# Differential attention in a hand-written matmul order, with the layer's last projections between its blocks

## The chip, the cores and the metric

The program runs on one core of a Trainium2 chip. The metric is the device time of one execution in microseconds (us). The engines are named as in the profile: PE (TensorE; PEld its weight loads), DVE (VectorE), ACT (ScalarE), POOL (GpSimd) and SP (SyncE, which issues the DMAs here).

## What is computed

A block of three branches (RWKV, convolution, memory attention) runs first; then two layers of this form, on a sequence of 1024 rows of width 1024. The change touches only these two layers.

```
for layer in range(2):
    h = rms_norm(x, norm_pre[layer])
    proj = h @ w_in[layer]                       # 4128 columns
    (gq, gk, gv, gg, gaf, gab, dq, dk, dv, dg, hq, hzf, hzb, hi, hg) = split(proj)
    y_a = gla_branch(...)                        # a scan forward and one backward, norm, * silu(gg)
    y_b = diff_branch(dq, dk, dv, dg, ...)
    y_c = hgrn_branch(...)                       # two scans, norm, * silu(hg)
    x = x + rms_norm(concat([y_a, y_b, y_c]) @ w_out[layer], norm_post[layer])

def diff_branch(q, k, v, g, ...):                # 4 heads, each with two pairs q, k of width 64
    q, k = rope(q) * 64**-0.5, rope(k)
    for each block of 128 queries:
        p = softmax(q @ k^T)                     # both pairs, over all 1024 keys
        w = p[0] - lam * p[1]
        o = w @ v                                # v is 128 wide
    o = rms_norm(o, norm_w) * (1 - lambda_init)
    return o * silu(g)
```

## The kernel before

Everything is float32. A projection is split in high and low parts, three matmuls for one (`mm3`): weights `whi` and `wlo` (made by ACT and by DVE or POOL from `wraw`), activations `hh` and `hl` in `hT`. One projection makes 128 columns for 1024 rows in two halves of 512; a half is 24 matmuls of 128x512 into one PSUM bank of the pool `fl`, and an evacuation follows: `p_func` copies it out by ACT, `p_rope` by ACT, then DVE and POOL, and `p_silu_le` reads the bank three times (ACT, DVE, DVE at its end). The result goes to DRAM.

A layer is `layer()`: six projections first, then `scans()`, `diff()` and the layer's output (`layer_out`, which reads all of `hT`). The other projections are a queue, `layer_stream`, from which `Stream.burst()` gives a part of one: `step` = 4 of the 8 row blocks, 12 matmuls, called a burst here. `scans()` has three scans (GLA, two pairs of HGRN heads); each has `scan_levels` (many small matmuls `aps`) and `scan_out` (state, outputs `ops`, norm sums `fst` in `finish_head`). Within these the PE order is pinned (`pinned`, `pin`: program order), and bursts stand between, all but each 14th call (`SKIP`). `reach(n)` runs the queue until n items are left. What remains at the end is fed at once by `stream.feed(1000)`, unpinned. Where nothing is pinned, a planner that runs when the program is built sets each engine's order. Scan outputs go to DRAM as float32 (`d_y`).

`diff()` then runs 32 blocks: four heads (`attend` twice per head) of eight blocks of 128 queries. A block is `weights` (eight score matmuls `sc` of 128x512 with the helper tiles `qz`, two maxima on DVE, two exps on ACT into `p`, a reciprocal and two combining steps on DVE), then eight transposes `wt` in two halves with two ACT copies into `wT`, then eight products `o_ps`. Four blocks make a half; it is normed (four squares on ACT, then Ln, Exp and a DVE product), transposed (`otp`), gated and put in `hT` as high and low parts. The next head's operands are loaded and split by `diff_qk` and `diff_v`, and between the halves `split_in` loads the scan outputs and splits them into `hT`. PSUM: two tiles for scores, three for `wt`, one for `o_ps`. Nothing of this is pinned.

## Time and profile before

| what | value |
|---|---|
| three runs | 3854.43, 3858.89 and 3860.61 us |
| median | 3858.89 us |
| profiled execution | 3856.55 us, span 3854.7 us |
| PE busy | 3531.4 us, 92% |
| layer 0: scans / rest to the layer's output | 348.21 / 232.13 us |
| layer 1: scans / rest to the layer's output | 350.14 / 239.70 us |

The median is 2.3 us longer than the profiled execution. A window is a stretch of the span in us, with each engine's busy time in it, the mean granted clock of PE (1.00 is 2.4 GHz), and the share and rate of DMA. A group puts instructions of one line and form together. A wait is idle time of an engine, with the instruction whose end released it.

### The profile page before, as it was taken

The numbers are of one execution on the slowest core, as the hardware profiler recorded it, in microseconds if no ns is written. First come the engines' busy times: TensorE is split into PE (matmuls) and PEld (weight loads), VectorE is DVE, ScalarE is ACT, GpSimd is POOL, SyncE is SP. The second block draws the span as 40 slices with busy tenths as digits, with TensorE's granted clock in tenths as the row PEclk, the third lists the DMA queues.
The fourth block names the chain that finished last, engine by engine and source line by source line (L and its number), as shares of the span: only waits on it lengthen the run. The fifth ranks groups of instructions, "written<-read, shape, count | busy, mean of one in ns | idle before, by whom it ended". The sixth has DMA issues, their size and how long they took to land. (4 is left out here: it accounts for less than half of the span.)

```text
span 3854.7 us, 69637 instructions
## 1 busy us (share of the span) xinstructions
PE 3531.4 (92%) x27522; PEld 2766.1 (72%) x27522; DVE 2330.0 (60%) x4505; ACT 1898.7 (49%) x3445; POOL 824.4 (21%) x710
## 2 busy tenths in 40 slices
PE   7999999999999999998999999899889999898887
PEld 5877766667666667766788767677777677677776
DVE  4346677777767767655454545465784544665863
ACT  4334544444444444445342445564674444655762
POOL 1002333333333333332122300012211300022111
PEclk9999999999999999999999999999999999999898
DMA  4421222222222222236554452323201442323113
GB/s 149 148 91 60 87 79 82 76 79 76 84 71 87 79 84 78 86 122 220 191 170 139 140 170 99 111 81 102 93 31 62 148 133 83 105 97 104 53 38 108
DMA packets 222584, 394.63 MB, mean 102 GB/s; under 512 B 24624, under 2 KB 44080, under 8 KB 222128
## 3 DMA queue, kind: packets, MB, share of 16 engines
q1 hardware_dynamic: 222256, 390.17, 30.4%
q8 instruction: 216, 3.54, 0.4%
q14 instruction: 112, 0.92, 0.1%
HBM read 268.44 MB, written 121.63 MB: 101 GB/s over the span
## 5 line engine op out<-in xcount | busy, mean ns | idle before, releaser
L250 PE MATMUL ps<-hh,whi 128*128 128x512 f32 (+2 forms) x3056 | 1280.5, 419 | 30.1 <-DVE st L202 11.8
L250 PE MATMUL ps<-hh,wlo 128*128 128x512 f32 (+2 forms) x3056 | 1200.4, 393 | 5.0 <-DVE wlo L202 4.9
L250 PE MATMUL ps<-hl,whi 128*128 128x512 f32 (+2 forms) x3056 | 1199.0, 392 | 4.2 <-DVE hl L202 4.2
L250 PEld LDWEIGHTS ps<-hh,whi 128*128 128x128 f32 (+1 forms) x3056 | 581.2, 190 | 198.7 <-issue 30.5
L250 PEld LDWEIGHTS ps<-hh,wlo 128*128 128x128 f32 (+1 forms) x3056 | 581.5, 190 | 137.8 <-DVE wlo L202 6.8
L250 PEld LDWEIGHTS ps<-hl,whi 128*128 128x128 f32 (+1 forms) x3056 | 583.1, 191 | 130.9 <-issue 19.7
L199 ACT ACTIVATE whi<-wraw 128x512 fp32r<-128x512 f32 x486 | 302.6, 625 | 556.9 <-PE ps L250 430.9
L202 DVE TENSOR_TENSOR wlo<-wraw,whi 128x512 fp32r<-128x512 f32 x398 | 296.5, 749 | 384.6 <-ACT whi L199 344.1
L202 POOL TENSOR_TENSOR uacg<-uacg,ut 128x512 f32<-128x512 f32 x240 | 339.0, 1413 | 781.5 <-ACT ut L569 646.2
L202 POOL TENSOR_TENSOR st<-st,rope 128x512 f32<-128x512 f32 x64 | 91.5, 1449 | 861.8 <-DVE st L415 855.0
L199 ACT ACTIVATE st<-ps 128x512 f32<-128x512 f32 (+2 forms) x260 | 149.3, 574 | 242.1 <-PE ps L250 213.4
L573 DVE SCALAR_TENSOR_TENSOR uacc<-uh,vecs,uacc 128x512 f32<-128x512 f32 x224 | 205.8, 919 | 8.1 <-ACT uacc L565 7.2
L202 POOL TENSOR_TENSOR acc<-acc,sq 128x512 f32<-128x512 f32 (+1 forms) x91 | 126.0, 1393 | 296.5 <-ACT sq L199 295.2
L202 POOL TENSOR_TENSOR wlo<-wraw,whi 128x512 fp32r<-128x512 f32 x88 | 121.0, 1375 | 287.1 <-ACT whi L199 260.3
L1387 DVE TENSOR_REDUCE D<-sc 128x1 f32<-128x1024 f32 x128 | 154.6, 1220 | 36.4 <-PE sc L250 36.1
L569 ACT ACTIVATE ut<-uh,vecs 128x512 f32<-128x512 f32 x240 | 166.0, 715 | 4.4 <-POOL uacg L202 3.7
L199 ACT ACTIVATE p<-sc,D 128x1024 f32<-128x1024 f32 x128 | 142.5, 1114 | 37.9 <-DVE D L1387 37.0
L250 PE MATMUL o_ps<-h,wT 128*128 128x128 f32 x1024 | 134.8, 280 | 12.9 <-ACT wT L199 12.9
L250 PEld LDWEIGHTS o_ps<-h,wT 128*128 128x128 f32 x1024 | 128.9, 195 | 22.6 <-ACT wT L199 17.5
L250 PE MATMUL sc<-h,h 128*128 128x512 f32 x256 | 96.3, 458 | 43.1 <-ACT p L199 43.1
L1380 POOL CAST qz<-h 64x128 fp32r<-64x128 f32 x128 | 53.8, 420 | 315.4 <-PE sc L250 309.0
L250 PE MATMUL ps<-oh,wlo 128*128 128x512 f32 x256 | 103.8, 406 | 4.6 <-DVE wlo L202 4.6
(331 smaller groups left out, 5885.4 us busy)
## 6 DMA issues: line engine op xcount, KB each, us to landing
wraw<-in_w_in_dram SPq DMA_DIRECT2D x326, 256.0 KB, 2.8
wraw<-in_w_out_dram SPq DMA_DIRECT2D x76, 256.0 KB, 2.7
g<-st SPq DMA_DIRECT2D x48, 256.0 KB, 2.2
y<-st SPq DMA_DIRECT2D x48, 256.0 KB, 2.0
gt<-y SPq DMA_DIRECT2D x48, 256.0 KB, 3.0
wraw<-in_w_mem_kv_dram SPq DMA_DIRECT2D x32, 256.0 KB, 2.9
yp<-gt SPq DMA_DIRECT2D x32, 256.0 KB, 3.3
yt<-yp SPq DMA_DIRECT2D x32, 256.0 KB, 3.1
```

What stands on the lines that cost most here:

```text
L199: self.nc.scalar.activation(out=out, in_=in_, func=func, **kw)
L202: (eng or self.nc.vector).tensor_tensor(out=out, in0=a, in1=b, op=op)
L250: self.pin(self.nc.tensor.matmul(out, lhsT=lhsT, rhs=rhs, start=start, stop=stop))
L569: keep(nc.scalar.activation(out=t, in_=u[:, j:j + 512], func=AF.Copy, scale=w(j)))
L573: keep(nc.vector.scalar_tensor_tensor(out=acc, in0=u[:, k:k + 512], scalar=w(k), in1=acc, op0=ALU.mult, op1=ALU.add))
L1380: nc.gpsimd.tensor_copy(out=Qz[slot][c][HEADS[c]], in_=Qs[c][HEADS[c], ts_])
L1387: nc.vector.reduce_max(out=D[:, c:c + 1], in_=sc, axis=AX.X, negate=True)
```

## The change

The queue of projections no longer ends ahead of the attention. `scans()` stops it at eight left (a `NEED` table says how many may be left at which place; `SKIP` is 4), and `diff(l, stream)` runs the rest in bursts of six matmuls (`step` = 2), pinned between its own. All matmuls of the attention are pinned too. Scores are written two blocks ahead (`LOOK`), so six `p` tiles are kept. PSUM in the attention: one bank for projections, two for `wt` instead of three. Two of the four gates of the attention (`g2`, `g3`) come later in the queue, and `g4` and `g5` last. `hT` is needed by projections to the end of the queue, so scan outputs and early heads are split at once and stored in DRAM as two tensors (`keep_out`), and `kept()` loads them into `hT` once the queue is empty. The rope tables are loaded again in the attention. The norm of a half is now one DVE product, one square, a DVE sum and a POOL product.

```diff
-FIRST, SKIP, PV = 6, 14, 5
+FIRST, SKIP, PV = 6, 4, 5
-NEED = 10
+NEED = dict(scan=18, qk=14, v=13, scans=8, heads=(5, 2), gates=(1, 0))
+LOOK = 2
...
-        for hd in range(4):
-            yield S(DG + hd, f"g{2 + hd}")
         for hd in range(4):
...
             yield P(DV + hd, f"d{hd}v")
+            for j in {1: (0, 1), 3: (2, 3)}.get(hd, ()):
+                yield S(DG + j, f"g{2 + j}")
...
+    def keep_out(self, p, o, j, sl):
+
+        hi, lo = p.tile([128, 512], F32, tag="fr", name="yhi", bufs=2).bitcast(R32), o.bitcast(R32)
+        self.act(hi, o)
+        self.lo(lo, o, hi)
+        for d, t in zip(self.d_y, (hi, lo)):
+            self.nc.sync.dma_start(out=d[j, :, sl], in_=t.bitcast(F32))
...
-            p1, p2, p3 = pool("d1", 1), pool("d2", 2), pool("d3", 5)
-            opp, wtp, scp = pool("dop", 1, space=PSUM), pool("dwt", 3, space=PSUM), pool("dsc", 2, space=PSUM)
+            p1, p2, p3 = pool("d1", 1), pool("d2", 2), pool("d3", 2 * LOOK + 2)
+            opp, wtp, scp = pool("dop", 1, space=PSUM), pool("dwt", 2, space=PSUM), pool("dsc", 2, space=PSUM)
+            self.fl = pool("dfl", 1, space=PSUM)
+            self.rot = self.rope(p1, ("rot0", "rot1"))
+            self.step, self.pinned = 2, True
...
-                for tt in range(4):
-                    self.act(o[:, tt], o_ps[:, tt], AF.Square, scale=D[:, tt, 4:5], accum_out=r[:, tt:tt + 1])
+                self.mul(o, o_ps, four(D[:, :, 4]))
+                self.act(q, o, AF.Square)
+                nc.vector.reduce_sum(out=r[:, 0:4], in_=q, axis=AX.X)
                 self.act(r[:, 4:8], r[:, 0:4], AF.Ln, scale=1.0 / 128, bias=self.eps(0))
                 self.act(r[:, 4:8], r[:, 4:8], AF.Exp, scale=-0.5)
-                self.mul(r[:, 4:8], r[:, 4:8], D[:, :, 4])
-                self.mul(o, o_ps, r[:, 4:8].rearrange("p (n o) -> p n o", o=1).to_broadcast([128, 4, 128]))
+                self.mul(o, o, four(r[:, 4:8]), eng=nc.gpsimd)
+                return o
...
                 self.stt(g, tp, nw, g, ALU.mult, ALU.mult)
-                self.put(self.hT[2 + hd], sl, g)
...
+                if stream.q or stream.g:
+                    self.keep_out(p1, g, 2 + hd, sl)
+                    waits.append((2 + hd, sl))
+                else:
+                    self.put(self.hT[2 + hd], sl, g)
+
+            def kept():
+                for j, sl in [(j, sl) for j in LAST[:4] for _, sl in self.halves()] + waits:
+                    for d, t in zip(self.d_y, self.hT[j]):
+                        nc.sync.dma_start(out=t[:, sl].bitcast(F32), in_=d[j, :, sl])
...
+            for b in range(LOOK):
+                ahead(b)
+                share(2 * b + 2)
+            pending = None
+            o_ps, held_back = None, True
+            for b in range(32):
+                hd, half, tt = b // 8, b // 4 % 2, b % 4
+                if b + LOOK < 32:
+                    ahead(b + LOOK)
+                goal = 4 + (b + 1) * 44 / 18 if b < 18 else 48 + 2 * (b - 17)
+                share((done + goal) / 2)
+                wT = turned(P.pop(b))
+                if pending and tt == 1:
+                    if pending[1] >= 2:
+                        reach(NEED["gates"][pending[1] - 2])
+                    out(*pending)
+                    pending = None
+                share(goal)
...
+                for kt in range(8):
+                    self.mm(o_ps[:, tt], wT[:, kt], vt[:, kt], kt == 0, kt == 7)
+                if tt == 3:
+                    pending = normed(o_ps, Ds[b // 4]), hd, slice(half * 512, half * 512 + 512)
...
+                if held_back and not (stream.q or stream.g):
+                    kept()
+                    held_back = False
+            out(*pending)
+            self.step, self.pinned = 4, False
...
                 if i == 0:
                     stream.reach(left)
+                elif i == 1:
+                    stream.reach(NEED["scan"])
...
-            self.pinned = False
-            self.head0 = qk, self.diff_v(0, l, self.qt, "t")
-            stream.feed(1000)
+            stream.reach(NEED["v"])
+            self.head0 = qk, self.diff_v(0, l, None, self.qt, "t")
+            stream.reach(NEED["scans"])
+            self.pinned = False
...
-                    nc.sync.dma_start(out=self.d_y[j, :, sl], in_=o)
+                    self.keep_out(p1, o, j, sl)
```

What this moves is seen on PE and DVE. First PE, some blocks into the first head of layer 0's attention, before; `sc` are scores, `wt` transposes, `o_ps` products:

```order
L250 MATMUL o_ps<-h_26249,wT 128x128 x8
L253 MATMUL wt<-const,p 128x128 x8
L250 MATMUL sc<-h_25769,h_25767 128x512 x2
L250 MATMUL sc<-h_25770,qz_26558 128x512 x2
L250 MATMUL sc<-h_25768,h_25766 128x512 x2
L250 MATMUL sc<-h_25770,qz_26559 128x512 x2
L250 MATMUL o_ps<-h_26249,wT 128x128 x8
```

In the changed kernel PE has this in the same head (`ps` are projections):

```order
L253 MATMUL ps<-hh_101,whi 128x512
L253 MATMUL ps<-hl_102,whi 128x512
L253 MATMUL ps<-hh_101,wlo 128x512
L256 MATMUL wt<-const,p 128x128 x8
L253 MATMUL ps<-hh_87,whi 128x512
L253 MATMUL ps<-hl_88,whi 128x512
L253 MATMUL ps<-hh_87,wlo 128x512
L253 MATMUL ps<-hh_89,whi 128x512
L253 MATMUL ps<-hl_90,whi 128x512
L253 MATMUL ps<-hh_89,wlo 128x512
L253 MATMUL o_ps<-h_25971,wT 128x128 x8
L253 MATMUL sc<-h_25523,h_25521 128x512 x2
```

Before, one block's transposes follow the last one's products at once, and the scores stand between them and their own products; now six projection matmuls stand ahead of the transposes and six more between them and the products, and the scores behind the products are those of two blocks later.

Then PE in the last quarter of layer 0's attention in the changed kernel, where the queue is empty:

```order
L253 MATMUL o_ps<-h_27578,wT 128x128 x8
L253 MATMUL sc<-h_27491,h_27489 128x512 x2
L253 MATMUL sc<-h_27493,qz_26033 128x512 x2
L253 MATMUL sc<-h_27492,h_27490 128x512 x2
L253 MATMUL sc<-h_27493,qz_26034 128x512 x2
L256 MATMUL wt<-const,p 128x128 x8
L256 MATMUL otp<-const,os 128x128 x4
L253 MATMUL o_ps<-h_27578,wT 128x128 x8
```

No projection stands between transposes and products there, and the output's transposes `otp` stand between them in one block of four.

Last DVE, at the gating of a half in layer 0's attention, before; `D<-sc` are maxima, `ld` is the gated half:

```order
L1387 TENSOR_REDUCE D<-sc 128x1
L202 TENSOR_TENSOR or<-or,D 128x4
L202 TENSOR_TENSOR os<-o_ps,or 128x512
L1387 TENSOR_REDUCE D<-sc 128x1
L1391 RECIPROCAL D<-D 128x2
L208 SCALAR_TENSOR_TENSOR ld<-otp,nw,ld 128x512
L208 SCALAR_TENSOR_TENSOR D<-D,lt 128x1
L208 SCALAR_TENSOR_TENSOR p<-p,D 128x1024
```

And in the changed kernel, where a silu's two DVE steps (`st`) now pass there:

```order
L211 SCALAR_TENSOR_TENSOR ld<-otp,nw,ld 128x512
L205 TENSOR_TENSOR ld<-ld,yhi 128x512
L211 SCALAR_TENSOR_TENSOR st<-ps,st 128x512
L1407 TENSOR_REDUCE D<-sc 128x1 x2
L205 TENSOR_TENSOR st<-st,ps 128x512
L1411 RECIPROCAL D<-D 128x2
L211 SCALAR_TENSOR_TENSOR D<-D,lt 128x1
L211 SCALAR_TENSOR_TENSOR p<-p,D 128x1024
```

Two maxima stand between the silu's first step and its product, which is the last read of the projection's bank; the split of the gated half (`ld` and `yhi`) stands ahead of both.

## Rows read from the trace of the kernel before

**Rows 1.** Page, part 1: busy time, share and instructions of each engine.

```profile
PE 3531.4 (92%) x27522; PEld 2766.1 (72%) x27522; DVE 2330.0 (60%) x4505; ACT 1898.7 (49%) x3445; POOL 824.4 (21%) x710
```

**Rows 2.** Windows by stage: from:to, length, busy time of each engine (instructions), clock, DMA.

```profile
2341.94:2690.15 348.21, 323.59 (x4138) 257.52 (x4138) 200.54 (x323) 195.52 (x307) 35.53 (x24) 0.98 0.28 94
2690.15:2922.28 232.13, 200.02 (x1235) 171.97 (x1234) 173.67 (x247) 165.49 (x350) 35.56 (x72) 0.96 0.18 59
3143.24:3493.38 350.14, 322.61 (x4137) 256.82 (x4137) 206.22 (x331) 195.07 (x307) 35.52 (x24) 0.98 0.28 93
3493.38:3733.08 239.70, 206.26 (x1235) 176.31 (x1234) 173.58 (x247) 165.53 (x350) 38.53 (x72) 0.93 0.17 58
```

**Rows 3.** Windows inside layer 0: first levels, first outputs, other scans, tail, start-up, blocks.

```profile
2341.94:2437.84 95.90, 92.28 (x1210) 73.53 (x1210) 46.23 (x75) 42.29 (x66) 0.00 (x0) 0.96 0.23 79
2437.84:2506.70 68.86, 55.46 (x794) 43.06 (x792) 36.09 (x53) 49.30 (x75) 0.00 (x0) 0.94 0.39 126
2506.70:2690.15 183.45, 175.85 (x2138) 140.94 (x2138) 118.22 (x195) 103.93 (x168) 35.53 (x24) 0.99 0.26 90
2690.15:2723.80 33.65, 33.65 (x153) 27.70 (x152) 11.36 (x22) 9.33 (x18) 11.65 (x12) 1.00 0.33 114
2723.80:2744.50 20.70, 13.61 (x56) 10.14 (x55) 18.71 (x27) 18.14 (x32) 2.64 (x7) 0.84 0.39 130
2744.50:2918.60 174.10, 152.26 (x1026) 133.62 (x1024) 142.74 (x197) 136.01 (x291) 21.26 (x53) 0.97 0.12 40
```

**Rows 4.** Windows inside layer 1: start-up of the attention, and its blocks.

```profile
3527.04:3548.40 21.36, 13.45 (x53) 10.07 (x51) 17.49 (x25) 16.89 (x30) 3.10 (x6) 0.72 0.37 127
3548.40:3729.50 181.10, 158.74 (x1030) 138.14 (x1028) 143.90 (x199) 137.31 (x293) 23.77 (x54) 0.94 0.12 40
```

**Rows 5.** Window in layer 0's tail, projection matmuls on PE alone.

```profile
2693.00:2720.00 27.00, 26.97 (x118) 1.00 0.29 96
```

**Rows 6.** Window of one block of attention without a gap on PE.

```profile
2749.88:2754.39 4.51, 4.51 (x35) 1.00 0.17 60
```

**Rows 7.** PE's waits, layer 0's scans, then attention: total, times, longest, us.

```profile
PE fst L250 <- ACT fr L199: 11.9, 2, 10.5
PE ps L250 <- DVE st L202: 5.2, 2, 3.6
...
PE sc L250 <- ACT p L199: 21.2, 14, 3.1
PE o_ps L250 <- ACT wT L199: 6.1, 7, 1.5
PE otp L253 <- DVE os L202: 3.3, 2, 3.2
```

**Rows 8.** Groups in layer 0's blocks: xcount | busy us, mean ns | idle.

```profile
L1387 DVE TENSOR_REDUCE D<-sc 128x1 f32<-128x1024 f32 x57 | 68.6, 1219 | 14.0 <-PE sc L250 13.9
L199 ACT ACTIVATE p<-sc,D 128x1024 f32<-128x1024 f32 x58 | 64.5, 1113 | 17.0 <-DVE D L1387 16.5
L208 DVE SCALAR_TENSOR_TENSOR p<-p,D 128x1024 f32<-128x1024 f32 x30 | 38.5, 1284 | 0.9
L199 ACT ACTIVATE wT<-wt 128x512 f32<-128x512 f32 x62 | 34.9, 597 | 13.5 <-PE wt L253 13.4
L202 DVE TENSOR_TENSOR h<-st,h 64x512 fp32r<-64x512 f32 x17 | 11.8, 693 | 2.9 <-ACT h L199 2.5
```

**Rows 9.** Timeline: start us, us, engine; first and last step of one silu.

```profile
2515.93 0.60 ACT L199 ACTIVATE st<-ps 128x512 f32<-128x512 f32 x1 [0.70 <-PE ps L250]
...
2519.72 0.68 DVE L202 TENSOR_TENSOR st<-st,ps 128x512 f32<-128x512 f32 x1
```

**Rows 10.** Timeline of layer 0's start-up: PE's longest wait, and ACT then.

```profile
2739.15 1.22 PE L250 MATMUL sc<-h,h 128*128 128x512 f32 x2 [3.08 <-ACT p L199]
...
2732.69 5.17 ACT L199 ACTIVATE h<-st 64x512 fp32r<-64x512 f32 x8
```

**Rows 11.** Page, part 5: the POOL product of 128x512.

```profile
L202 POOL TENSOR_TENSOR st<-st,rope 128x512 f32<-128x512 f32 x64 | 91.5, 1449 | 861.8 <-DVE st L415 855.0
```

More of the change, by code (lines that the diff above doesn't have):

```diff
@@ L1281, in layer @@
             self.scans(l, stream)
-            self.diff(l)
+            self.diff(l, stream)
     def held(self, i, dt=F32):
@@ L1346, in rope, with diff @@
         return r
-    def diff(self, l):
+    def diff(self, l, stream):
         nc, tc = self.nc, self.tc
@@ L1413, in attend, with normed @@
+            four = lambda a: a.rearrange("p (n o) -> p n o", o=1).to_broadcast([128, 4, 128])
+            def normed(o_ps, D):
                 o = p2.tile([128, 4, 128], F32, tag="os", name="os")
+                q = p1.tile([128, 4, 128], F32, tag="oq", name="oq")
                 r = p2.tile([128, 8], F32, tag="or", name="or")
-                for tt in range(4):
-                    self.act(o[:, tt], o_ps[:, tt], AF.Square, scale=D[:, tt, 4:5], accum_out=r[:, tt:tt + 1])
+                self.mul(o, o_ps, four(D[:, :, 4]))
+                self.act(q, o, AF.Square)
+                nc.vector.reduce_sum(out=r[:, 0:4], in_=q, axis=AX.X)
@@ new lines, in kept, with ahead @@
+            def kept():
+                for j, sl in [(j, sl) for j in LAST[:4] for _, sl in self.halves()] + waits:
+                    for d, t in zip(self.d_y, self.hT[j]):
+                        nc.sync.dma_start(out=t[:, sl].bitcast(F32), in_=d[j, :, sl])
+            cur = {0: self.head0}
+            Ds, P = {}, {}
+            def ahead(b):
+                hd, half, tt = b // 8, b // 4 % 2, b % 4
+                if tt == 0:
+                    Ds[b // 4] = p3.tile([128, 4, 8], F32, tag="D", name="D")
+                (Qs, Kd, kl), _ = cur[hd]
+                P[b] = weights(Qs, Kd, kl, half * 512 + tt * 128, Ds[b // 4][:, tt])
@@ new lines, in diff, with share, reach @@
+            done, total = 0, 8 * NEED["scans"]
+            def share(n):
+                nonlocal done
+                while done < n and (stream.q or stream.g):
+                    stream.burst()
+                    done += 1
+            def reach(left):
+                nonlocal done
+                stream.reach(left)
+                done = max(done, total - 8 * left)
+            for b in range(LOOK):
+                ahead(b)
+                share(2 * b + 2)
+            pending = None
```

65 lines of the change are left out of this document (32 added, 33 removed).

## The prediction

> **What bounds the kernel now.** Read the engine totals first: PE is busy for 3531.4 of 3854.7 us, DVE for 2330.0 [rows 1]. So a change gains by removing PE's idle time or its work; the matmuls stay the same here, which leaves idle time. Next come the windows by stage. Nothing in the change touches the instructions ahead of 2341.94 us, nor those from 2922.28 to 3143.24 and after 3733.08. What it touches are four stretches, the scans and the attention of either layer: 348.21 + 232.13 + 350.14 + 239.70 = 1170.2 us [rows 2]. In the scans PE works 323.59 of 348.21 us; in the stretch with the attention 200.02 of 232.13 and 206.26 of 239.70, and there it also runs at a lower granted clock, 0.96 and 0.93 against 0.98 [rows 2]. That stretch splits into four [rows 3]: a tail of pure projections (33.65 us, PE full), a start-up of 20.70 us with 13.61 us of PE, the blocks (174.10 us, PE 152.26), and the end of the last norm. In layer 1 the start-up takes 21.36 us at clock 0.72 and the blocks 181.10 at 0.94 [rows 4].
>
> To see how much of it is wait, I lay the dense cost beside it. Projection matmuls run 118 in 27.00 us, 0.2288 each [rows 5], so a burst of 12 is 2.74 us. A block run without a gap (scores, turned weights, products with the values) takes 4.51 us [rows 6]. Per layer then: 12 bursts 32.9, 32 blocks 144.3, and about 6 for the transposes of heads and outputs (estimate from the same records): 183.2 us. The rest, **48.9 us in layer 0 and 56.5 in layer 1**, is waits and lower clock. The grouped waits name the largest: scores for an exp 21.2 us in 14 places, products for a copy of the turned weights 6.1 in 7 [rows 7]. DVE has 142.74 us of work in the blocks and ACT 136.01 [rows 3], so neither lies far below PE's 152.26.
>
> **What the scans give back.** By the two orders the scans and their tail issue 26, 12, 13, 10, 13, 12 and 12 bursts per layer before. After, they issue 21, 9, 11, 8, 11 and 8, and 30 go into the attention: 18 leave the scans (49.4 us of PE), 12 come from the tail. The first level stage is dense (92.28 of 95.90) and DVE has only 46.23 there, so its five bursts are worth 13.7 in full. One wait in the scans for a silu's DVE product (5.2 us in two places [rows 7]) has its silu later now: 0.9 for that. In the first output stage PE idles 13.4 us of 68.86 and ACT works 49.30 [rows 3]; the longest wait there is for ACT ahead of a norm's sum, 10.5 us [rows 7]. Removing three bursts (8.2) gives between 0 and 8.2, since ACT's chain is next; I take half, 4.1. The other two scans have PE at 175.85 of 183.45 [rows 3]; ten bursts leave (27.4). They give at most 27.4, and at least what is left if ACT's and DVE's chains in the two output stages (six bursts, 16.5) return nothing: 10.9. Following those chains I take 22.9. Sum **41.6 us per layer, bounds 25 to 50**.
>
> **What the attention costs.** PE work: 30 bursts 82.3 + blocks 144.3 + 7 = 233.6 us. Added are waits, which the fixed order now places. I went through the new orders block by block with the durations of [rows 8 to 11]:
> - *Boundary and start-up, 9.3.* The lambda matmul that opens the attention waits for DVE and ACT to finish the last scan output, now with its split ahead of it (an ACT copy of 0.65 [rows 10] and a DVE subtraction of 0.69 [rows 8]): 3.8, an estimate from these and the product, the gate and the two lambda products of the chain. Then ACT makes the next head's operands, eight copies 5.17 us together, while PE waited 3.08 [rows 10]; now bursts stand between the first scores. I take 5.5; the bounds are 0 and the 7.1 that PE idles in the start-up of before (20.70 − 13.61). The rope tables are loaded a second time (two loads on SP) ahead of the head's loads; that is within the bound.
> - *The single bank for projections, 6.7.* Scans have two `fl` banks, the attention one. Fifteen half projections pass, so 14 times the next one's first burst waits until ACT has copied the last one out (0.6). Between them usually stand scores, transposes or products, so most crossings cost 0.3 to 0.9. One, in head 0's second half, where the next head's copies queue on ACT ahead of it, costs 4.6.
> - *Silus that hold that bank, 11.6.* The last two projections are gates. A silu reads its bank until DVE's product ends: from 2515.93 to 2520.40, 4.5 us when nothing is in the way [rows 9]. In the new DVE order the next block's two maxima (2 × 1.22 [rows 8]) stand ahead of that product, on ACT an exp stands between. Three crossings: 2.5 + 3.6 + 5.5. Bounds: 0 if the block between covers all, 3 × 7 = 21 if nothing does.
> - *Filled blocks otherwise, 7.1* (short switches between shapes 2.4, small waits 4.7; estimates). A filled block is 4.51 + 2.74 = 7.25 us of PE, against roughly 5.8 of DVE and 5.2 of ACT (186 and 167 us over 32 blocks, from the work of before [rows 2] with what moves in and out). So the waits for an exp go: scores are two blocks ahead, and six projection matmuls stand between the transposes and the products.
> - *Last eight blocks, 8.5.* There the stream is empty, and PE's order is scores, transposes, products. The copies of the turned weights (two of 0.597 [rows 8]) lie bare in every block; before, the planner put other scores there. DVE's 2 × 1.219 + 1.284 with its small ones and a share of the norms [rows 8] asks for nearly as much. So a period of some 5.6 instead of 4.51.
> - *End, 4.3.* The last norm now has a DVE product, one square, a sum and a POOL product of 1.45 [rows 11] in its chain; before, PE waited 3.2 there [rows 7].
>
> Waits together 47.5, stretch **281.1 us** per layer.
>
> At no cost: the split of the scan outputs is the ACT copy and DVE subtraction that the blocks did before, now in the scans, under their projections; the doubled stores and the reloads into `hT` (SP, some 28 loads of 256 KB per layer behind the stream's end) lie under the last eight blocks, since the DMA share in the blocks is 0.12 [rows 3]. If that cover fails, the layer's output projection starts late, by about 3 us.
>
> **The sum** against the profiled execution, 3856.55 us: layer 0 (281.1 − 232.1) − 41.6 = +7.4, layer 1 (281.1 − 239.7) − 41.6 = −0.2, together **+7.2, so 3864**. The median of the three runs is 2.3 us longer than the profiled one; that is below what a measurement of this kernel can tell (0.2%, 7.7 us), so I leave it. The break-even: waits of 43.9 us per layer; measurably slower from 47.8, faster below 40.
>
> The row on the single bank is that of the silu wait, 5.2 us in two places even with two banks [rows 7]. The Trainium skill ("Perfetto Trace Analysis", Matmuls) says that independent groups of matmuls should rotate through different PSUM banks, so that one's evacuation overlaps the next one's matmuls; the new attention doesn't. By that rule all 14 crossings are exposed, which is the second rival. The same page (Optimization Strategy) says that stages with different busiest engines may gain from being interleaved; the tail (DVE 11.36 of 33.65) and the blocks (142.74 of 174.10) are such a pair [rows 3], and the third rival is that result.
>
> **The rivals.**
> 1. *The waits that I placed by hand are covered* (faster). ACT's copies come in time for every crossing, so 6.7 goes to 0. The silus cost 1.5 each, 4.5 in all; boundary and start-up 5.5. Then 29.9 us per layer, 2 × (29.9 − 43.9) = −28: 3829. For it: ACT is free 38 us in the blocks of before. Against: it is in order, and an exp of 1.113 [rows 8] may stand ahead of any copy.
> 2. *The single bank starves PE* (slower). Of the eleven plain crossings five wait as long as the longest score for its exp in before, 3.1 us (the mean is 21.2 / 14 = 1.5) [rows 7], because ACT's copy stands behind the exps that now run two blocks ahead; I have 0.6 for each of them. That is 5 × 2.5 = 12.5 us per layer over my sum, 25 in all: 3889. It decides early: the kernel is measurably slower from 47.8 us of waits, 0.3 over my 47.5. For it: in the fixed order nothing else can run on PE then. Against: most crossings have a block's scores or products between them.
> 3. *Everything is filled* (much faster): only switches, end and a few waits are left, 13 us per layer: 2 × (13 − 43.9) = −62, 3795. Against: the last eight blocks have no filler.
> 4. *The change doesn't do what it says in the scans*: their output stages and the level stages hang on ACT's and DVE's chains, so the scans shrink by only 27 us per layer. 2 × 14.6 over my sum: 3893. Against: PE is dense in the level stages [rows 3].
>
> **How the numbers follow.** Forecast 0.38 (3850 to 3878: faster by over 0.2% for 0.01, within for 0.24, slower for 0.13), rival 1 0.27, rival 3 0.07, rival 2 0.20, rival 4 0.08. Faster by over 0.2%: 0.27 + 0.07 + 0.01 from the lower end of the forecast = 0.35. Within: 0.24. Slower: 0.13 + 0.20 + 0.08 = 0.41. The range leaves out rival 3 and the outer ends of rivals 1, 2 and 4: 3815 to 3900; the forecast's own is 3850 to 3878.
>
> **What would show it.** In the changed kernel's windows, each layer's scans should take 306 to 309 us, the attention with its projections 281. PE's waits for an exp should almost vanish, and waits of projections for ACT's copy and DVE's silu product should take their place, largest at the gates (2.5 to 5.5 each). The last eight blocks should have a period near 5.6 us. I am wrong if the scans stay over 320, if the crossings sum to under 5 or over 30 us per layer, or if the attention's stretch is under 270.

## The result, and the profile after

The changed kernel takes 3967.7 us against 3857.7: a ratio of **1.0285 (95% interval 1.0267 to 1.0303)**, 110 us slower. The forecast was 3864, the range 3815 to 3900; the result is outside, on the slow side.

First the engine totals on the page of the changed kernel:

```profile
PE 3568.2 (90%) x27522; PEld 2795.4 (71%) x27522; DVE 2355.7 (59%) x4505; ACT 1884.6 (48%) x3333; POOL 823.1 (21%) x726
```

PE does the same number of matmuls and is busy 36.8 us longer than the 3531.4 of before [rows 1]. The work is the same, so its matmuls ran slower; the rest of the 109.7 us of longer span is idle time. Next the windows. To compare like with like I cut each layer behind the last norm sum of the scans, not at 2690.15 as [rows 2] did, since 4.3 us of projections stand before that point. The changed kernel: scans, boundary up to the lambda matmul, attention, for layer 0 and then for layer 1 (columns as in [rows 2]).

```profile
2344.04:2678.44 334.40, 288.99 (x3921) 228.85 (x3920) 191.86 (x301) 180.70 (x282) 23.25 (x17) 0.92 0.25 87
2678.44:2687.87 9.43, 2.33 (x9) 1.43 (x8) 3.19 (x8) 4.10 (x9) 3.77 (x6) 0.58 0.43 144
2687.87:2983.07 295.20, 254.19 (x1438) 215.59 (x1438) 193.46 (x261) 168.80 (x310) 45.66 (x82) 0.94 0.27 90
3201.97:3538.84 336.87, 288.34 (x3921) 227.95 (x3920) 197.18 (x309) 180.33 (x282) 23.34 (x17) 0.92 0.26 86
3538.84:3547.94 9.10, 2.32 (x10) 1.43 (x9) 3.19 (x8) 4.11 (x9) 3.75 (x6) 0.57 0.41 145
3547.94:3846.43 298.49, 255.63 (x1438) 216.97 (x1439) 193.49 (x261) 168.87 (x310) 45.19 (x82) 0.93 0.27 89
```

The kernel before with the same cut, scans and the rest:

```profile
2341.94:2685.86 343.92, 319.30 (x4119) 254.12 (x4119) 198.48 (x320) 193.53 (x303) 35.53 (x24) 0.98 0.28 92
2685.86:2921.80 235.94, 203.83 (x1251) 174.89 (x1249) 175.73 (x250) 167.48 (x353) 35.56 (x72) 0.96 0.19 63
3143.24:3489.16 345.92, 318.39 (x4119) 253.45 (x4119) 204.17 (x328) 193.08 (x303) 35.52 (x24) 0.98 0.27 91
3489.16:3732.70 243.54, 210.10 (x1251) 179.31 (x1249) 175.63 (x250) 167.52 (x353) 38.53 (x72) 0.93 0.18 61
```

| layer 0 / layer 1, us | before | after | moved | forecast length | missed by |
|---|---|---|---|---|---|
| scans | 343.9 / 345.9 | 334.4 / 336.9 | −9.5 / −9.0 | 306.6 / 308.5 | 27.8 / 28.4 |
| rest, to the last output transposes | 235.9 / 243.5 | 304.6 / 307.6 | +68.7 / +64.1 | 281.1 / 281.1 | 23.5 / 26.5 |

The forecast lengths are 348.21 − 41.6 and 350.14 − 41.6 for the scans and 281.1 for the rest. They are compared as lengths and not as moves, because [rows 2] counts before's 4.3 us of projections to the scans and this cut counts them to the rest; in the changed kernel no projection stands there. Both lines miss, in the same direction: 28 us per layer in the scans, 24 and 27 in the rest. The four moves sum to +114; the other parts of the program are 4.5 us shorter. Among them, the stretch from layer 0's last output transposes to layer 1's first scan takes 218.9 us against 221.4, so the reloads into `hT` didn't delay what follows.

Then PE's waits in layer 0, the scans first, then from the boundary on (total, times, longest, us):

```profile
PE fst L253 <- ACT fr L202: 22.2, 3, 11.6
PE ops L253 <- ACT os L202: 9.3, 3, 4.4
PE ps L253 <- DVE st L205: 5.2, 2, 3.1
...
PE otp L256 <- ACT wT L202: 11.1, 7, 5.1
PE ps L253 <- DVE st L205: 11.0, 3, 5.3
PE sc L253 <- ACT p L202: 6.3, 2, 5.7
PE tp L256 <- DMA st<-d0v: 4.8, 2, 3.2
PE ps L253 <- ACT st L202: 4.7, 4, 2.5
PE o_ps L253 <- ACT wT L202: 3.8, 9, 1.0
```

The waits for an exp are down from 21.2 us in 14 places [rows 7] to 6.3 in 2, as the change intends. In their place stand ACT's copies of turned weights ahead of `otp`, silus' products, the load of head 0's values, and in the scans the norm sums (22.2 us in 3 places against 11.9 in 2 [rows 7]).

One of these waits close up. ACT's rows first (start us, us), then PE's:

```profile
2752.20 5.21 ACT L202 ACTIVATE h<-dl 64x512 fp32r<-64x512 f32 x8 [3.01 <-PE sc L253]
2757.44 1.11 ACT L202 ACTIVATE p<-sc,D 128x1024 f32<-128x1024 f32 x1
...
2760.15 1.08 ACT L202 ACTIVATE wT<-wt 128x512 f32<-128x512 f32 x2
...
2753.40 0.40 PE L253 MATMUL ps<-hh,whi 128*128 128x512 f32 x1
2753.63 0.40 PE L253 MATMUL ps<-hl,whi 128*128 128x512 f32 x1
...
2754.80 1.03 PE L256 MATMUL wt<-const,p 128*128 128x128 f32 x8
2760.89 1.09 PE L256 MATMUL otp<-const,os 128*128 128x128 f32 x4 [5.06 <-ACT wT L202]
2761.63 0.78 PE L253 MATMUL ps<-hh,whi 128*128 128x512 f32 x1
2762.20 0.63 PE L253 MATMUL ps<-hl,whi 128*128 128x512 f32 x1
2762.63 0.63 PE L253 MATMUL ps<-hh,wlo 128*128 128x512 f32 x1
```

ACT makes head 1's operands (eight copies, 5.21 us) ahead of the block's exps, so the copies of the turned weights come at 2760.15 and PE stands 5.06 us. And behind the wait the projection matmuls come every 0.43 to 0.57 us instead of 0.23. The granted clock between 2760.89 and 2764.30 is 0.50, in the matmuls ahead of the wait (2753.40 to 2754.80) it is 1.00. So the wait costs its own 5.06 us and, estimated from these spacings, about another 2 in slower matmuls.

The longest silu wait in the attention, ACT, DVE and PE. The silu's first step reads the bank at 2916.47, DVE's last one at 2921.82; PE resumes at 2922.56. Between them ACT has another exp and two copies of weights in its queue, DVE a reciprocal and the block's combining step:

```profile
2916.47 0.59 ACT L202 ACTIVATE st<-ps 128x512 f32<-128x512 f32 x1
...
2918.64 1.28 DVE L211 SCALAR_TENSOR_TENSOR p<-p,D 128x1024 f32<-128x1024 f32 x1
2920.43 0.69 DVE L211 SCALAR_TENSOR_TENSOR st<-ps,st 128x512 f32<-128x512 f32 x1 [0.51 <-ACT st L202]
2921.82 0.69 DVE L205 TENSOR_TENSOR st<-st,ps 128x512 f32<-128x512 f32 x1 [0.69 <-ACT st L202]
...
2916.20 1.03 PE L256 MATMUL wt<-const,p 128*128 128x128 f32 x8
2922.56 0.79 PE L253 MATMUL ps<-hh,whi 128*128 128x512 f32 x1 [5.33 <-DVE st L205]
```

### The profile page after: what moved, and what is told of

Same layout as the page of the kernel before. It is cut to its first block, busy times and chain, and to the rows that moved or that the text cites. A ratio compares the mean times of both kernels' runs of the same rounds, so it can differ in the third digit from the quotient of the medians.

```text
span 3964.4 us, 69682 instructions
## 1 busy us (share of the span) xinstructions
PE 3568.2 (90%) x27522; PEld 2795.4 (71%) x27522; DVE 2355.7 (59%) x4505; ACT 1884.6 (48%) x3333; POOL 823.1 (21%) x726
## 3 DMA queue, kind: packets, MB, share of 16 engines
q1 hardware_dynamic: 233200, 411.15, 31.1%
## 4 chain that ended last, share of the span: by engine, by line
PE 61%; DVE 18%; ACT 9%; DMA 6%; issue 4%; POOL 1%; SPq 0%; DVEq 0%; POOLq 0%; ACTq 0%
PE ps L253 43%; PE o_ps L253 3%; PE sc L253 3%; PE tps L253 2%; PE ch L253 2%; DVE uacc L577 2%; ACT st L202 2%; PE g L253 1%; PE aps L253 1%; DVE h L205 1%; ACT p L202 1%; ACT h L202 1%; DVE tm L205 1%; DVE st L211 1%; DVE T L205 1%
## 5 line engine op out<-in xcount | busy, mean ns | idle before, releaser
L1407 DVE TENSOR_REDUCE D<-sc 128x1 f32<-128x1024 f32 x128 | 152.8, 1218 | 69.1 <-PE sc L253 68.7
L573 ACT ACTIVATE ut<-uh,vecs 128x512 f32<-128x512 f32 x240 | 166.0, 715 | 4.4 <-POOL uacg L205 3.5
L1400 POOL CAST qz<-h 64x128 fp32r<-64x128 f32 x128 | 42.3, 331 | 394.2 <-PE sc L253 393.5
L205 DVE TENSOR_TENSOR h<-h,tot 128x512 f32<-128x512 f32 x120 | 84.2, 736 | 39.7 <-ACT kk L202 38.1
```

The costliest lines, as they stand in the source:

```text
L205: (eng or self.nc.vector).tensor_tensor(out=out, in0=a, in1=b, op=op)
L573: keep(nc.scalar.activation(out=t, in_=u[:, j:j + 512], func=AF.Copy, scale=w(j)))
L1400: nc.gpsimd.tensor_copy(out=Qz[slot][c][HEADS[c]], in_=Qs[c][HEADS[c], ts_])
L1407: nc.vector.reduce_max(out=D[:, c:c + 1], in_=sc, axis=AX.X, negate=True)
```

## The experiments

Three things came together in the change: bursts leave the scans (thinning), outputs are split in the scans (split), and the attention takes the bursts in a pinned order (order). The runs do and undo them. The attention's new form (two blocks ahead, the banks, the norm) comes with the order in every run that has it; no run separates it. Each ratio is against runs of before made beside it, whose medians lie between 3852.4 and 3858.6 us, so a difference of a few us is read from the ratios. Stage lengths are taken from the starts of PE's groups in each run's timeline, layer 0 / layer 1, in us; "levels" are the three level stages, "outputs" the three output stages, "rest" the boundary and the attention with all bursts that run from there on. The cut is the last norm sum, and where the planner puts a different number of projections ahead of it, the text says so.

| run | ratio (95%) | levels | outputs | rest |
|---|---|---|---|---|
| before | 1 | 186.6 / 187.2 | 157.4 / 158.7 | 235.9 / 243.5 |
| after | 1.0285 (1.0267–1.0303) | 169.8 / 172.7 | 164.6 / 164.2 | 304.6 / 307.6 |
| thin_only | 1.0157 (1.0140–1.0173) | 167.6 / 167.5 | 154.7 / 155.7 | 290.1 / 290.1 |
| out_bare | 1.0400 (1.0370–1.0431) | 171.9 / 169.3 | 124.9 / 124.8 | 363.1 / 359.6 |
| split_only | 1.0059 (1.0042–1.0075) | 188.6 / 190.9 | 171.3 / 172.5 | 234.9 / 235.9 |
| store_twice | 1.0020 (1.0006–1.0033) | 185.0 / 189.5 | 159.2 / 161.0 | 236.1 / 238.4 |
| split_off | 1.0230 (1.0208–1.0252) | 168.0 / 175.2 | 156.9 / 153.4 | 303.4 / 304.2 |
| scans_dense | 1.0119 (1.0099–1.0140) | 187.3 / 190.5 | 165.9 / 168.5 | 249.3 / 253.9 |
| silu_copied | 1.0142 (1.0124–1.0161) | 165.7 / 169.6 | 166.0 / 165.0 | 280.8 / 283.1 |
| before_silu | 1.0021 (1.0010–1.0032) | 185.2 / 186.9 | 162.3 / 162.9 | 235.2 / 235.8 |
| loose | 1.0046 (1.0029–1.0062) | 168.3 / 170.6 | 166.2 / 172.4 | 255.8 / 253.0 |
| loose_whole | 1.0003 (0.9993–1.0013) | 166.8 / 170.3 | 155.1 / 155.7 | 261.3 / 257.2 |
| dense_loose_whole | 0.9905 (0.9885–0.9925) | 187.0 / 188.8 | 157.5 / 161.6 | 221.6 / 221.1 |
| dense_loose_whole_silu | 0.9882 (0.9864–0.9900) | 184.8 / 185.6 | 160.4 / 161.2 | 221.3 / 225.3 |

My theory after the result had two forms: A, the split is what kept the scans long; B, thinning itself returns little there. thin_only, split_only, split_off and scans_dense were to tell them apart.

### thin_only: thinning alone

```diff
--- before
-FIRST, SKIP, PV = 6, 14, 5
+FIRST, SKIP, PV = 6, 4, 5
-NEED = 10
+NEED = dict(scan=18, qk=14, v=13, scans=8, ...)
...
+            stream.reach(NEED["v"])
+            self.head0 = qk, self.diff_v(0, l, self.qt, "t")
+            stream.reach(NEED["scans"])
             self.pinned = False
-            self.head0 = qk, self.diff_v(0, l, self.qt, "t")
             stream.feed(1000)
```

> The kernel before with one part of the change: bursts leave the scans as in the changed kernel (its order of the queue, its NEED and SKIP), and run in the unpinned tail ahead of the attention; outputs stay whole in DRAM and the attention is the old one. Each layer's tail grows by 18 bursts, 49.4 us. Theory A (the split of the outputs in the scans' output stages is what kept the scans from shrinking): the scans shrink by about 31 us per layer here, so the kernel takes 3858 + 2 x 18 = about 3895. Theory B (thinning itself returns little, because the output stages hang on chains of ACT and DVE and PE only waits more in them): the scans shrink by 17 or less, and the kernel takes 3920 to 3945. What I forecast (41.6 back) would give about 3874.

Measured 3913.0 us, a ratio of 1.0157: between the two. Nine bursts (24.7 us) that leave the level stages return 19.0 us, but the seven and a half (20.4) that leave the output stages return 2.7. The scans shrink by 21.6 at this cut, not by 37.3 (the 41.6 of the forecast without the 4.3 us of projections), and not by theory A's 31. What became of the rest is in the window of layer 0's scans:

```profile
2344.50:2666.84 322.34, 285.18 (x3922) 226.38 (x3922) 186.24 (x294) 177.04 (x275) 22.02 (x16) 0.94 0.24 84
```

At 0.2288 us each [rows 5] the matmuls that left are 45.1 us of PE, but PE is busy only 34.1 us less than before's 319.30: its clock is 0.94 against 0.98. And it idles 37.2 us against 24.6. So of the 23.5 us that don't come back about 11 are slower matmuls and 12.5 are waits.

### out_bare: no bursts in the output stages

```diff
--- thin_only
-                self.scan_out(cur, l, self.V(...), burst)
+                self.scan_out(cur, l, self.V(...), lambda: None)
```

> The run thin_only with no burst at all inside the three output stages of the scans; the bursts that stood there (about 25 per layer, 69 us of PE) run in the tail. It measures what a burst in an output stage is worth. If these stages hang on the chains of ACT, DVE and DMA, they keep their length (64, 44 and 47 us in thin_only) within some 3 us each, and the kernel takes 3913 + 2 x 60 or more, 4030 to 4050. If PE's work sets them, they shrink by 20 us or more each, and the kernel stays within 3913 to 3935. In between, the ratio is the share of a burst that is exposed there.

Measured 4008 us (1.0400; two executions), between the two expectations. The output stages of layer 0 go from 154.7 to 124.9 us for 25 bursts (68.6 us of PE): 0.43 us back for each us taken out. Their windows, thin_only and then out_bare:

```profile
2428.00:2492.28 64.28, 51.22 (x758) 40.12 (x756) 30.68 (x44) 40.39 (x60) 0.00 (x0) 0.87 0.34 115
2535.18:2579.14 43.96, 35.14 (x430) 27.24 (x428) 25.91 (x35) 22.95 (x34) 7.02 (x6) 0.94 0.24 81
2620.34:2666.84 46.50, 37.42 (x430) 29.97 (x429) 21.28 (x31) 33.08 (x52) 0.00 (x0) 0.93 0.17 57
```

```profile
2428.10:2479.88 51.78, 33.31 (x650) 24.42 (x648) 24.97 (x35) 28.89 (x41) 0.00 (x0) 0.62 0.23 74
2523.74:2560.77 37.03, 17.62 (x333) 13.73 (x332) 17.71 (x25) 18.00 (x25) 0.00 (x0) 0.72 0.10 33
2605.26:2641.34 36.08, 18.90 (x338) 14.56 (x337) 13.08 (x17) 21.10 (x31) 2.33 (x2) 0.72 0.10 36
```

Without any burst PE is busy 33.31 of 51.78 us in the first, about half of the others, at a clock of 0.62 to 0.72. ACT and DVE too are busy for only half. So it is a chain across the engines that holds these stages, and no engine's total, and a burst that stands in one costs less than half of itself as measured. The clock is part of that measure: thin_only has 0.87 to 0.94 in the same stages. By the trace's records of the granted clock, whose mean is the clock column of the windows, 49.0 of the 69.8 us in which PE is busy here are at the lower level, against 20.9 in thin_only. At nearly twice the time for each matmul (0.43 against 0.23 us above) that is up to 13 us of length, so with thin_only's clock the share could be as high as 0.62, an estimate.

### split_only: the split alone

```diff
--- before
...
-                    self.split_in(self.d_y[LAST[hd]], self.hT[LAST[hd]], sl)
+                    for d, t in zip(self.d_y, self.hT[LAST[hd]]):
+                        nc.sync.dma_start(out=t[:, sl].bitcast(F32), in_=d[LAST[hd], :, sl])
...
-                    nc.sync.dma_start(out=self.d_y[j, :, sl], in_=o)
+                    self.keep_out(p1, o, j, sl)
```

> The kernel before with one part of the change: the scan outputs are split in the scans and stored as two tensors, and the attention loads them straight into hT; order of the queue, bursts and attention as before. Theory A: every output stage is longer by 3 to 6 us, about 12 per layer, and the attention gains a little from the work that left it; about 3875 to 3885. Theory B: under the projections that still stand there the split costs nothing, and it takes work off the attention: 3845 to 3862.

Measured 3874.7 us (1.0059): the output stages grow by 13.9 and 13.8 us per layer. But the last of them holds 145 projection matmuls where before has 126: the planner placed 19 more, 4.3 us, ahead of the later norm sum, and they are gone from the rest, which is 1 us shorter in layer 0 (7.6 in layer 1). So the split itself costs 9.6 and 9.5 us per layer there, a little under theory A's 12; theory B's free split is ruled out, and both theories were half right.

### store_twice: the stores without the split

```diff
--- split_only
-        hi, lo = p.tile([128, 512], F32, tag="fr", name="yhi", bufs=2).bitcast(R32), o.bitcast(R32)
-        self.act(hi, o)
-        self.lo(lo, o, hi)
-        for d, t in zip(self.d_y, (hi, lo)):
-            self.nc.sync.dma_start(out=d[j, :, sl], in_=t.bitcast(F32))
+        for d in self.d_y:
+            self.nc.sync.dma_start(out=d[j, :, sl], in_=o)
```

> The run split_only with the split itself left out: the scan output is stored whole in both tensors, so the DMAs and the reloads are the same and the ACT copy and the DVE subtraction of each half are gone (the layer's output is computed from unsplit values, so it differs). If the split's work in ACT's and DVE's chains lengthens the output stages, they go back to before's 69, 44 and 45 us, and the kernel takes 3850 to 3860. If the buffers that wait for a second store do it, it stays at 3868 to 3878.

Measured 3859.6 us (1.0020). The output stages, split_only and then store_twice:

```profile
2434.15:2507.26 73.11, 59.28 (x793) 46.33 (x791) 38.23 (x56) 50.74 (x78) 0.00 (x0) 0.87 0.37 126
2553.63:2601.61 47.98, 40.66 (x453) 31.64 (x451) 27.10 (x43) 24.18 (x37) 12.08 (x8) 0.96 0.25 87
2647.90:2698.07 50.17, 46.18 (x482) 36.98 (x481) 24.00 (x37) 29.61 (x46) 12.40 (x8) 1.00 0.34 114
```

```profile
2437.32:2507.08 69.76, 56.90 (x793) 44.25 (x791) 36.06 (x53) 49.15 (x75) 0.00 (x0) 0.93 0.40 132
2553.65:2598.20 44.55, 41.20 (x454) 32.92 (x452) 25.38 (x41) 23.53 (x36) 12.12 (x8) 0.96 0.22 77
2643.08:2687.99 44.91, 41.11 (x459) 32.91 (x458) 21.91 (x34) 27.44 (x42) 12.38 (x8) 1.00 0.27 95
```

This kernel leaves the split out, so its output is computed from unsplit values. 73.11, 47.98 and 50.17 us become 69.76, 44.55 and 44.91, within 1 us of before, and the 19 projection matmuls are back behind the norm sum. So of the 9.6 us 7.7 (12.0 less the 4.3 of projections) are the ACT copy, the DVE subtraction or the shared `fr` buffer they use; the second store or a buffer that waits for it can be at most the other 1.8. Which of those, no run here separates; a buffer of its own for the copy wasn't tried.

### split_off: the change without the split

```diff
--- after
...
-                for j, sl in [(j, sl) for j in LAST[:4] for _, sl in self.halves()] + waits:
+                for j, sl in [(j, sl) for j in LAST[:4] for _, sl in self.halves()]:
+                    self.split_in(self.d_s[j], self.hT[j], sl)
+                for j, sl in waits:
...
-                    self.keep_out(p1, o, j, sl)
+                    nc.sync.dma_start(out=self.d_s[j, :, sl], in_=o)
```

> The changed kernel with whole scan outputs: stored as one tensor as before, loaded and split into hT when the queue of projections is empty. Theory A: the output stages shrink by about 12 us per layer; 3967 - 24 and some loss in the last blocks, about 3945. Theory B: the scans stay within 4 us of the changed kernel's, and ACT's and DVE's added work in the last eight blocks makes it 3965 to 3985.

Measured 3941.6 us (1.0230), 0.5% under the changed kernel: the split costs here about what it cost in split_only. The scans are 9.5 and 8.3 us per layer shorter, with the same projections in every stage. But with thinned scans and whole outputs it still is 28 us behind thin_only, whose attention is the old one. So moving the 30 bursts into this attention loses as well: rest 303.4 us against 290.1.

### scans_dense: the new attention with few bursts

```diff
--- after
-FIRST, SKIP, PV = 6, 4, 5
+FIRST, SKIP, PV = 6, 14, 5
-NEED = dict(scan=18, qk=14, v=13, scans=8, heads=(5, 2), gates=(1, 0))
+NEED = dict(scan=99, qk=10, v=9, scans=6, heads=(3, 0), gates=(3, 3))
...
-                goal = 4 + (b + 1) * 44 / 18 if b < 18 else 48 + 2 * (b - 17)
+                goal = 4 + (b + 1) * 24 / 17
```

> The changed kernel with the scans filled as before (SKIP 14, the old order of the queue), so that only 14 bursts are left for the attention, spread over its first 20 blocks; split outputs, fixed order and single bank as in the changed kernel. Theory A: the scans stay long, by the split: about 360 us per layer; the attention 14 x 2.74 + 151 + 47 = 237: in all about 3885. Theory B: scans of 348 to 352 us and the same attention: about 3860 to 3868. Under both the attention keeps waits of 40 us or more per layer.

Measured 3900.7 us (1.0119). That is above both theories. The scans are long by the split alone, 353 us in layer 0 and 359 in layer 1; 360 was right for layer 1. The rest takes 249.3 us, 13 more than before with as many bursts, and 12 more than the 237 that I had put into both theories (253.9 in layer 1).

### silu_copied: the projection's bank freed early

```diff
--- after
-            t = self.staged()
-            self.act(t, ps, AF.Abs)
+            t, x = self.staged(), self.staged()
+            self.act(x, ps)
+            self.act(t, x, AF.Abs)
...
-            self.mul(t, t, ps)
+            self.mul(t, t, x)
```

> The changed kernel with one more ACT copy in a silu's evacuation: the projection's bank is copied to SBUF first, and the silu works on the copy, so its bank is free after 0.6 us and not after DVE's last product. If silus that hold the single bank cost what the trace of the changed kernel shows (11.1 us of waits in layer 0's attention, 5.2 in its last output stage, and the lower clock behind each), it takes 3967 - 2 x 14 = about 3940, at best 3930. If ACT's queue is what holds PE, the extra copies give it back: 3960 to 3970.

Measured 3909.2 us (1.0142), 58 us under the changed kernel (55 by the ratios), twice the expected gain. Rest shrinks by 23.8 and 24.5 us in the two layers, where the silu waits of layer 0 were 11.0; the level stages give 3 to 4 more. PE's busy time in the attention falls with them, from 254.2 to 248.9 us, and its clock rises from 0.94 to 0.96; the wait for the first exps falls from 6.3 to 3.3 as the planner orders ACT anew. So of the 24 us about half is the wait itself, a quarter slower matmuls, the remainder other waits.

### before_silu: the same copy in the kernel before

The same edit on the kernel before, whose projections have two banks in the scans and no silu in the attention.

```diff
--- before
-            t = self.staged()
-            self.act(t, ps, AF.Abs)
+            t, x = self.staged(), self.staged()
+            self.act(x, ps)
+            self.act(t, x, AF.Abs)
...
```

> The kernel before with silus that copy their bank out first, and nothing else. It tells how much of silu_copied's 58 us comes from the single bank of the attention, and how much from silus anywhere: if from the single bank, this is within 8 us of before (3850 to 3862); if silus cost as much with two banks, it is 20 us or more faster.

Measured 3867.3 us (1.0021, interval 1.0010 to 1.0032): 8.8 us slower and so just outside the 8, the outputs by 4 to 5 us per layer. So what silu_copied saves belongs to the single bank in the pinned attention. This bears on the rule of the Trainium skill ("Perfetto Trace Analysis", Matmuls) that independent groups of matmuls should rotate through PSUM banks: the traces agree with it in the pinned order, 58 us with one bank there and none with the two of the scans. The number of banks was not varied by itself, and the next run has one bank too and no such wait.

### loose: the attention not pinned

```diff
--- after
-            self.step, self.pinned = 2, True
+            self.step, self.pinned = 2, False
```

> The changed kernel with the attention not pinned: the planner sets PE's order there, with the same pieces, the same banks, the same split. Moving 30 bursts per layer from a tail into the attention costs 28 us by split_off against thin_only. If the fixed order is the cause (PE waits at its head for one late operand while others are ready), this takes 3967 - 28 = 3940 or less. If the single bank and the queues of ACT and DVE are the cause, it stays at 3955 to 3980.

Measured 3870.0 us (1.0046): **2.4% back by one word**, far below the expected 3940. Boundary and attention of layer 0, and PE's largest waits there:

```profile
2675.18:2687.78 12.60, 8.65 (x38) 7.05 (x36) 3.45 (x10) 4.53 (x10) 0.49 (x1) 0.86 0.60 190
2687.78:2931.01 243.23, 229.68 (x1387) 199.01 (x1386) 192.70 (x257) 166.46 (x306) 57.33 (x82) 0.98 0.30 102
```

```profile
PE sc L253 <- ACT p L202: 4.0, 3, 2.2
PE tp L256 <- DMA st<-d0v: 3.9, 1, 3.9
PE o_ps L253 <- ACT wT L202: 2.3, 3, 1.8
PE ps L253 <- ACT st L202: 2.2, 1, 2.2
```

The same pieces, one bank, the same silus. PE is idle 17.5 us in 255.8 (3.95 + 13.55) against 48.1 in the pinned order, and busy 238.3 us against 256.5. Two bursts have moved ahead of the cut, 5.5 us; most of the rest of the 18 is the clock, 0.98 against 0.94 in the attention. The 5.3 us for a silu's product is gone from the list.

The word pins PE's matmuls alone, but the planner then orders ACT anew as well. In the changed kernel the eight copies for head 1 came at once; here they are parted, with a copy of turned weights between them:

```profile
2744.40 1.93 ACT L202 ACTIVATE h<-dl 64x512 fp32r<-64x512 f32 x3
...
2747.20 0.60 ACT L202 ACTIVATE wT<-wt 128x512 f32<-128x512 f32 x1
...
2749.01 2.60 ACT L202 ACTIVATE h<-dl 64x512 fp32r<-64x512 f32 x4
```

So the 2.4% is the price of pinning together with the queues that the planner builds around it; how much is PE's order alone is not shown.

### loose_whole: not pinned, and no split

Both edits, of loose and of split_off.

```diff
--- after
-            self.step, self.pinned = 2, True
+            self.step, self.pinned = 2, False
...
-                    self.keep_out(p1, o, j, sl)
+                    nc.sync.dma_start(out=self.d_s[j, :, sl], in_=o)
...
```

> The changed kernel with two parts undone: the attention is not pinned (as in loose) and the scan outputs stay whole (as in split_off). Thinned scans and 30 bursts per layer in the attention remain. If the parts add up, 3870 - 21 to 26 = 3844 to 3849, about 0.1 to 0.2% under the kernel before. If the late split of the outputs in the attention's last blocks takes the gain, 3860 to 3870.

Measured 3860.0 us (1.0003, interval 0.9993 to 1.0013): no difference from before. By the ratios it misses the sum of the parts by 5 to 9 us. The outputs return 11 and 17 us against loose, but 5.5 of each are the two bursts, which stand behind the cut again here: they make up the 5.5 and 4.2 us by which the rest grows. So no price of the late split is seen in the rest; the split returns 6 and 11 us, not the 21 to 26 together that I expected.

### dense_loose_whole and dense_loose_whole_silu: with the scans filled as before

scans_dense with the edits of loose and split_off; the second with silu_copied's too.

```diff
--- scans_dense
-            self.step, self.pinned = 2, True
+            self.step, self.pinned = 2, False
...
-                    self.keep_out(p1, o, j, sl)
+                    nc.sync.dma_start(out=self.d_s[j, :, sl], in_=o)
...
--- dense_loose_whole
-            t = self.staged()
-            self.act(t, ps, AF.Abs)
+            t, x = self.staged(), self.staged()
+            self.act(x, ps)
+            self.act(t, x, AF.Abs)
...
```

> As loose_whole, with the scans filled as before (SKIP 14, old order of the queue), so that 12 to 14 bursts per layer are left for the unpinned attention. What thinning showed: a burst is worth 2.1 us in a level stage, 0.3 in an output stage with others beside it, and its full 2.74 in a dense attention. By that the scans take 344 us as before and the attention with its bursts about 212 to 225 instead of 236: 3858 - 2 x (11 to 24) = 3810 to 3836. If it is the many bursts that fill the unpinned attention, its waits come back with 14: 3840 to 3860.

> As dense_loose_whole, with silus that copy their bank out first. The gates run in the scans here, which have two banks; the waits for a silu's product there are some 5 us in layer 0. Theory: 3 to 6 us per layer less than dense_loose_whole. Rival: ACT's added copies in the output stages, which hang on ACT, make it 2 to 6 us more.

Measured 3823.3 us (0.9905) and 3814.6 us (**0.9882, interval 0.9864 to 0.9900**). Both beat both kernels. The scans are about before's, and the rest is 221 to 225 us instead of 236 and 244 with the same bursts (scans_dense, pinned and split, has 249 and 254). Boundary and attention of layer 0 in the second:

```profile
2690.91:2912.17 221.26, 200.04 (x1250) 175.11 (x1249) 181.12 (x250) 160.19 (x297) 49.15 (x76) 0.96 0.26 86
```

For the added copy the two intervals overlap; levels shrink by 2 to 3 us, one output stage grows by 3. Its expected 3 to 6 us per layer isn't shown.

## Why the prediction was wrong

All numbers are of layer 0, unless said. There the four misses below are 15.7 + 12.1 + 22.9 + 0.6 = 51.3 us, which is the 27.8 and 23.5 of the table.

**What the scans give back: wrong, 16 us by thinning itself.** Forecast were scans of 306.6 us, thin_only has 322.3. For the first scan the steps held: thin_only returns 12.4 us in the levels where I said 13.7 and 0.9, and 4.6 in the first output stage where I said 4.1. The failing step is the other two scans, "Following those chains I take 22.9": thin_only returns 8.9, of which 4.3 are projections that stood behind the last norm sum, and that is also under my lower bound of 10.9. The two level stages give 6.6 for four bursts, and the output stages grow by 2.0 although they lose more than four. I had taken PE's 175.85 busy us of 183.45 as a sign that PE sets the time. It was only full because bursts filled it; out_bare shows what lies below, a chain that needs 36 to 37 us of each of these output stages with PE half idle, at the lower clock that this brings. And I let a burst that leaves take its full 2.74 us with it: over all scans thin_only lost about 11 us to the clock.

**"At no cost" for the split: wrong, 12 us.** I let the projections cover it. But ACT's copy and DVE's subtraction stand in the queues of the very chain that the output stages wait for, and the projections are on PE, which isn't that chain. The scans of the changed kernel are 12.1 us longer than thin_only's (334.4 against 322.3). By split_off, which differs in the split alone, 9.5 of them are the split, as in split_only (9.6 once the moved projections are taken off); store_twice put 7.7 of it on the split's own work. What the other 2.6 are is not shown.

**The attention's waits: right in sum, 47.5 forecast and 48.1 measured** (304.63 − 256.52 of PE). Piece by piece: the silus 2.5, 3.6 and 5.5 against 2.42, 3.30 and 5.33; the other crossings of the single bank 6.7 against 4.7; the start-up 5.5 against 6.3; the end 4.3 against 3.98; the last eight blocks 8.5 against about 6.5 (46.07 us from 2937.00 to 2983.07 with PE busy for 35.62, less the end). The boundary was too small, 3.8 against 7.1 us: DVE's lambda is 2.3 of it, and the load of head 0's values (4.8) isn't in my chain, since before it ran under the tail. In part the sum is luck: the boundary's 3.3 too few meet 4.0 too many in the bank and the last blocks. The 4.6 for head 1's copies is luck too: they do cost 5.06, but PE waits there for turned weights, with the output's transposes at its head, and not for the bank of the projections.

**PE's own time there: wrong, 23 us, the largest step.** I took 233.6 us at full clock, because bursts would fill the stretch; it is 256.5. The steady blocks do run dense. But behind the long waits the matmuls run at the lower of the two levels (1.2 of 2.4 GHz) at first, as the rows around 2761 and the 0.79 us matmul at 2922.56 show. The granted clock of the whole stretch is 0.93, and by its records 31.1 of the 256.5 us are at the lower level, worth about 15 by the spacings above. The other 8 are then a dense cost that was too low. Both stood in before: there PE is busy for 200.02 us [rows 2] where the dense cost was 183.2, 16.8 more (15.9 us are at the lower level, worth about 8), and in layer 1 23.1 more. I had counted this as wait, inside the 48.9 and 56.5, and put none of it into the new stretch: on one side of the sum alone. With the order free the reason half held: loose has 238.3 us with two bursts fewer.

**The rivals.** Rival 4 named the right place, and for thinning alone the right price: 27 us of 348.2, where thin_only gives 25.9. With the split on top the changed kernel gives 13.8, and I gave this rival 0.08. Rival 2 did not come as stated: PE's waits for ACT's copy out of the bank sum to 4.7 us in 4 places, the longest 2.5, and not five of 3.1. Of the 14 crossings seven show a wait, the silus' three among them. The rivals never asked what pinning itself costs. I compared the new order's waits with those of before, as if it were the bank that made them; loose has the same bank and little more than a third of the waits. The Trainium skill's advice to interleave stages with different busiest engines ("Perfetto Trace Analysis", Optimization Strategy) is borne out in these traces only once PE's order is free: from thin_only to loose_whole the bursts leave the tail for the attention in its new form, and the ratio falls from 1.0157 to 1.0003. By busy time the pair fits it loosely, as PE is the busiest engine in the tail and in the blocks [rows 3]; what the blocks had to offer is PE's waits.

Taken in this order of runs: thinning +1.57%, moving the bursts into the new, unpinned attention −1.54, the split +0.43, pinning +2.39; together the 2.85%.

What stays open: whether the copy, the subtraction or the shared buffer makes the split dear, what one bank costs by itself, how much of pinning's price is ACT's queue, and how much of pinning's price would remain with a better order by hand.

## What to carry to other kernels

A stage in which PE is nearly always busy may be full only because fillers were put there: before moving them away, ask how long the chain below needs, by a run without them. A hand-written order can turn a late operand into a wait of the engine at its head, so weigh it against the free order with the same pieces before any finer count. A wait costs more than its length where the clock falls behind it; so lay PE's busy time beside the dense cost in the kernel before, and carry the difference over. And compare stages at the same cut, with a count of the fillers in each.

## What the runs showed of the hardware

Behind a wait of 5.06 us the next projection matmuls came every 0.43 us at a granted clock of 0.50, against 0.23 at 1.00 ahead of it. The attention took 256.5 us of PE's busy time pinned and 238.3 (with two bursts fewer) unpinned. In output stages without bursts the granted clock was 0.62 to 0.72, with them 0.87 to 0.94, so the matmuls there run slower just where they are waited for: the fillers kept the clock up as well. Over all scans of a layer, taking out 45.1 us of matmuls brought PE's busy time down by 34.1.
